# Six edits of a three-block transformer kernel: gain row, mixer order, routing copies, loop rings, stick-breaking order, last norm

## The chip, the cores and the metric

One Trainium2 chip, one core of it. The metric is the device time of one execution in microseconds (us), the median of several runs. The engines are named as in the profile: PE is TensorE, DVE is VectorE, ACT is ScalarE, POOL is GpSimd, SP is SyncE, whose queue carries nearly all transfers.

## What is computed

256 tokens of width 1024, float32 throughout. Two layers, each a mixer and an expert layer with 16384 experts (`peer_ffn`); then one block of two kinds of attention and an MLP.

```python
# layer 0: x += even_mix(norm(x)); x += peer_ffn(norm(x))
# layer 1: x += fox_mix(norm(x));  x += peer_ffn(norm(x))
def rms_norm(x, g):
    return x * lax.rsqrt(jnp.mean(x * x, axis=-1, keepdims=True) + EPS) * g

def even_mix(h, ...):
    p = h @ w_in
    a_val, a_gate, q, k, v, r, glr = jnp.split(p, cuts, axis=-1)
    # gated, a 31-tap causal convolution over the tokens per channel, layer norm, silu
    y_a = conformer_conv(a_val, a_gate, conv_w, conv_b, ln_g, ln_b)
    o = gla_chunked(q, k, v, log_a)              # gated linear attention, 4 heads
    y_b = rms_norm(o, gla_norm_g) * jax.nn.silu(r)
    return jnp.concatenate([y_a, y_b], axis=-1) @ w_out

def peer_ffn(h, wq, keys, u, v):
    q = (h @ wq).reshape(B, S, 8, 2, 128)
    s1, s2 = ...                                 # q against 128 + 128 keys per head
    v1, i1 = lax.top_k(s1, 16); v2, i2 = lax.top_k(s2, 16)
    sc, j = lax.top_k(v1[..., :, None] + v2[..., None, :], 16)
    experts = i1[j // 16] * 128 + i2[j % 16]
    gates = jax.nn.softmax(sc, axis=-1)
    act = jax.nn.gelu(h . u[experts])
    return sum over experts of gates * act * v[experts]

def second_block(x, c, ...):
    mod = jax.nn.silu(c) @ ada_w + ada_b         # shifts, scales and gates
    z = (rms_norm(h) * (1 + scale1) + shift1) @ w_in
    y_a = nsa_attention(...) @ w_up_nsa
    y_b = stick_breaking_attention(q_b, k_b, v_b) @ w_up_sb   # 8 heads
    h = h + gate1 * ((sigmoid(m_a) * y_a + sigmoid(m_b) * y_b) @ w_out)
    u2 = rms_norm(h) * (1 + scale2) + shift2
    return h + gate2 * (square(relu(u2 @ mlp_w1)) @ mlp_w2)
```

## The kernel before

**Products.** Every large product is made of three, of a high and a low part of each operand (`H` and `L`), so that its result is as good as float32. A weight arrives by SP's queue in pieces of 128x1024 (512 KB). `wsplit` (line 110) makes the high part of a piece on ACT (line 90) and the low part on DVE or POOL (line 93). Which of the two is a matter of the ring from which the piece's tiles come: `K.rings` names for each ring, `u`, `v` and at times `w`, the pool and the engine of its low parts. A ring has two tiles of each part (`hu`, `lu`, `hv`, `lv`), so a piece's split waits until PE has finished with the piece two before it in the same ring. By default ring `u` has its low parts on POOL and ring `v` on DVE.

**Expert layer.** All experts are computed, and a matrix `G` (experts by tokens, zero for those not chosen) weighs them. Expert block n is 128 experts; there are 128 blocks in two halves of 64. `first(n)` is 24 matmuls (line 742) and a gelu on ACT (line 745, tile `A`); `gated(n)` multiplies by `G` on DVE (line 750, `AG`) and splits the product (`CH` on ACT, `CL` on DVE); `second(n)` is 12 matmuls per block (lines 764, 765, 768) into four PSUM banks `po`. `RUN` = 40 firsts run ahead of the gated products, and a second follows its gated product by `LAG` = 2 blocks.

**Routing** (line 605) chooses the experts while PE computes queries and, by `ahead`, some of the firsts. `top16` is a chain of DVE operations for each of 8 heads. Behind the last head four ACT copies (line 681, `xe`, 128x2048 each) spread the indices of all eight heads; a softmax and one-hot products on DVE follow (lines 700, 701, 708, 711), and PE transposes their results (lines 705, 713).

**Loop** (line 812). For each half, `spread` builds `G` by one-hot products on DVE (lines 785 to 790: `o1`, `o2`, `og`) and PE; all rings have their low parts on DVE until the loop over n begins, and the rings of before (`u` on POOL) from there on. In some steps of the loop 512 KB of the block's conditioning weights are loaded and multiplied on DVE (line 1035).

**First mixer** (`even`, line 386). The convolution is split: channel group 0 and the first `PART` taps of group 1 run on PE by diagonal matrices, the others on DVE as one operation per tap (line 525). The gated attention's last products (`po`), their norm (`osq`, `oss`) and transposes (line 572) follow the taps. **Norm** (`norm_rows`, line 227): sums of squares (line 207), scaling with the gain row (line 258), transposes on PE (line 261); `leave` and `take` add a mixer's result to `X` (line 318).

**Stick-breaking attention** in `block2`: for each of four pairs of heads `keep_probs` (logits, log-sigmoids `ls`, `lk`), `stick` (sums by a triangular matrix, line 1312, and an exponential) and `sb_values`, with products of the input projection (`wide`) between them; then a sigmoid of the two gates (line 1340, `mg`), two products up and the output product.

The compiler's scheduler orders instructions that aren't pinned, by a priority that follows the order of the code; each engine runs its own list in order.

Of the kernel before, what the change touches and what calls it, by code (L numbers as in the profile page):

```python
# [44 lines left out]
class Kit:  # L45


    def __init__(self, ctx, tc, I):
# [11 lines left out]
        nc.sync.dma_start(self.row, row_bc(I["ev_norm"]))  # L60
# [16 lines left out]
        self.warm(WARM)  # L77
# [149 lines left out]
    def norm_rows(self, g, shift=None, early=(), after=None):  # L227
# [8 lines left out]
        W, outs = [], []  # L236
        first = not self.carry
        rs = [self.rstd(tb, tb > 0) for tb in range(2)] if first else []
        for tb in range(2):
# [7 lines left out]
            if not tb:  # L247
                W = [self.wsplit(*w, (0,), nc.vector) for w in raw]
# [19 lines left out]
            if not tb:  # L268
                for (H, L), w in zip(W, raw):
                    for a, b in zip((H, L), self.wsplit(*w, (1,), nc.vector)):  # L270
                        a.extend(b)
# [110 lines left out]
CONV = (0, 0, 0, 8, 14, 14), (0, 0, 0, 2, 18, 22)  # L382
PART = 12


def even(K, side):
    tc, nc, I = K.tc, K.nc, K.I
    K.table()
    with tc.tile_pool(name="evz", bufs=1) as ez, ExitStack() as stack:
# [159 lines left out]
        K.rings = old  # L549
        last = conv_dve(len(steps))  # L550
# [5 lines left out]
        for tb in range(2):  # L556
            po = pm.tile([128, 4, 128], F, name="pm")
            for h in range(4):
                if tb:
                    nc.tensor.matmul(po[:, h], ATx[:, h], V[0][:, h], start=True, stop=False)  # L560
                nc.tensor.matmul(po[:, h], AT[tb][:, h], V[tb][:, h], start=not tb, stop=True)
            sq = wk.tile([128, 4, 128], F, name="osq")
            ss = wk.tile([128, 4], F, name="oss")
            nc.scalar.activation(sq, po, AF.Square)
            nc.vector.tensor_reduce(ss, sq, axis=AX.X, op=OP.add)
            nc.scalar.activation(ss, ss, AF.Ln, bias=K.eps, scale=1.0 / 128)
            nc.scalar.activation(ss, ss, AF.Exp, scale=-0.5)
            for h in range(4):
                nc.vector.scalar_tensor_tensor(sq[:, h], po[:, h], ss[:, h:h + 1], sr[tb][:, h], op0=OP.mult, op1=OP.mult)
            pt = pm.tile([128, 4, 128], F, name="pm")  # L570
            for h in range(4):
                nc.tensor.transpose(pt[:, h], sq[:, h], K.ident)
# [32 lines left out]
def routing(K, l, grid, rt, new_psum, e1T, e2T, gP, ahead):  # L605
# [31 lines left out]
    q = {}  # L637

    def evac(g, ps):
        q[g] = rt.turn("q", [128, S], bufs=4)  # L640
        nc.scalar.activation(q[g], ps, AF.Copy)
# [23 lines left out]

    qs = K.row[:, 0:512].rearrange("p (a b) -> p a b", b=256)
    nc.scalar.activation(qs, qn, AF.Copy)
    for h in range(1, 8):
        K.gemm_T(I[f"p{l}_wq"], (2 * h - 2, 2 * h), K.hH, K.hL, lambda g, ps: evac(g + 2, ps), psum=pfx)
        ahead(1)  # L670
        if h == 1:
# [5 lines left out]
            best(0)  # L677
        best(h)
    for t in range(2):
        for i in range(2):  # L680
            nc.scalar.activation(xe[:, t, :, i], IX[:, t, i::2, :, None].to_broadcast([128, 8, 16, 16]), AF.Copy)
# [899 lines left out]
```

## Time and profile before

| | |
|---|---|
| median of 3 runs | 2380.89 us (2379.44 to 2382.56) |
| the profiled execution's own time | 2386.93 us |
| its span, first to last instruction | 2385.2 us |
| mean granted TensorE clock | 0.987 |
| busy: PE, DVE, ACT, POOL | 97%, 66%, 53%, 34% of the span |

The device time holds the span and under 2 us around it. The profiled execution is 6 us above the median, so gains read from it are taken off the median, not off its own time. PE is busy nearly throughout; what can be won without taking away matmuls is the time in which it waits, and the time in which its granted clock is half.

### The profile page before, as it was taken

The numbers are of one execution on the slowest core, as the hardware profiler recorded it, in microseconds if no ns is written. First come the engines' busy times: TensorE is split into PE (matmuls) and PEld (weight loads), VectorE is DVE, ScalarE is ACT, GpSimd is POOL, SyncE is SP. The second block draws the span as 40 slices with busy tenths as digits, with TensorE's granted clock in tenths as the row PEclk, the third lists the DMA queues.
The fourth block names the chain that finished last, engine by engine and source line by source line (L and its number), as shares of the span: only waits on it lengthen the run. The fifth ranks groups of instructions, "written<-read, shape, count | busy, mean of one in ns | idle before, by whom it ended". The sixth has DMA issues, their size and how long they took to land.

```text
span 2385.2 us, 43282 instructions
## 1 busy us (share of the span) xinstructions
PE 2310.5 (97%) x16982; PEld 2092.9 (88%) x16982; DVE 1576.8 (66%) x3094; ACT 1260.9 (53%) x2031; POOL 801.7 (34%) x361
## 2 busy tenths in 40 slices
PE   8989899999999999999989999999999999999999
PEld 8879898988998988887989898899899879877997
DVE  5958997556873556644799756688355663657754
ACT  5544555555554555575455455555455554565542
POOL 4228304444003444552840344500244442323000
PEclk9999999999999999999999999999999999999999
DMA  7235446665556665642644576554566565334652
GB/s 248 80 116 182 138 142 218 241 203 188 167 168 206 235 214 194 214 141 70 196 139 147 195 245 206 192 176 154 194 239 225 195 214 177 115 105 152 213 188 94
DMA packets 119529, 425.15 MB, mean 178 GB/s; under 512 B 14170, under 2 KB 17052, under 8 KB 118940
## 3 DMA queue, kind: packets, MB, share of 16 engines
q1 hardware_dynamic: 119324, 422.38, 53.0%
q8 instruction: 133, 2.18, 0.4%
q14 instruction: 72, 0.59, 0.1%
HBM read 421.24 MB, written 2.66 MB: 178 GB/s over the span
## 4 chain that ended last, share of the span: by engine, by line
PE 45%; DVE 5%; issue 1%; ACT 1%; POOL 1%; POOLq 0%; ACTq 0%; DVEq 0%
PE pA L742 13%; PE pA L155 6%; PE po L764 5%; PE po L765 5%; PE po L768 5%; PE pB L155 2%; PE pB L799 1%; PE pA L196 1%; PE pA L197 1%; PE pA L195 1%; PE pB L197 1%; PE pB L195 1%; PE pB L196 1%; POOL lu L93 1%; DVE G L635 1%
## 5 line engine op out<-in xcount | busy, mean ns | idle before, releaser
L93 POOL TENSOR_TENSOR lu<-raw,hu 128x1024 fp32r<-128x1024 f32 x263 | 652.5, 2485 | 1198.0 <-ACT hu L90 1013.2
L90 ACT ACTIVATE hu<-raw 128x1024 fp32r<-128x1024 f32 x352 | 372.1, 1059 | 339.0 <-PE pA L742 251.0
L93 DVE TENSOR_TENSOR lv<-raw,hv 128x1024 fp32r<-128x1024 f32 x306 | 381.7, 1248 | 122.8 <-ACT hv L90 120.2
L90 ACT ACTIVATE hv<-raw 128x1024 fp32r<-128x1024 f32 x336 | 355.6, 1060 | 194.9 <-PE pA L742 81.2
L742 PE MATMUL pA<-hH,hu 128*128 128x256 f32 x1408 | 400.0, 284 | 5.2 <-ACT hu L90 5.2
L93 DVE TENSOR_TENSOR CL<-AG,CH 128x256 fp32r<-128x256 f32 x256 | 213.2, 834 | 288.6 <-PE po L768 167.1
L742 PE MATMUL pA<-hH,lu 128*128 128x256 f32 x1408 | 396.2, 281 | 6.4 <-POOL lu L93 6.1
L742 PE MATMUL pA<-hL,hu 128*128 128x256 f32 x1408 | 395.0, 281 | 0.0
L742 PEld LDWEIGHTS pA<-hH,lu 128*128 128x128 f32 x1408 | 269.6, 191 | 8.0 <-POOL lu L93 7.8
L742 PEld LDWEIGHTS pA<-hH,hu 128*128 128x128 f32 x1408 | 266.4, 189 | 9.2 <-ACT hu L90 6.0
L742 PEld LDWEIGHTS pA<-hL,hu 128*128 128x128 f32 x1408 | 267.4, 190 | 3.5
L90 ACT ACTIVATE CH<-AG 128x256 fp32r<-128x256 f32 x256 | 106.9, 419 | 296.9 <-PE po L765 280.5
L764 PE MATMUL po<-hv,CH 128*128 128x512 f32 x672 | 262.0, 390 | 0.0
L765 PE MATMUL po<-lv,CH 128*128 128x512 f32 x672 | 261.5, 389 | 0.0
L768 PE MATMUL po<-hv,CL 128*128 128x512 f32 x672 | 206.9, 389 | 0.0
L742 PE MATMUL pA<-hH,hv 128*128 128x256 f32 x640 | 184.5, 288 | 14.3 <-ACT A L745 14.3
L742 PE MATMUL pA<-hH,lv 128*128 128x256 f32 x640 | 180.0, 281 | 1.4 <-POOL lv L93 1.4
L742 PE MATMUL pA<-hL,hv 128*128 128x256 f32 x640 | 179.7, 281 | 0.0
L768 PEld LDWEIGHTS po<-hv,CL 128*128 128x128 f32 x672 | 126.2, 188 | 26.3
L764 PEld LDWEIGHTS po<-hv,CH 128*128 128x128 f32 x672 | 126.5, 188 | 22.8
L765 PEld LDWEIGHTS po<-lv,CH 128*128 128x128 f32 x672 | 126.4, 188 | 22.8
L765 PE MATMUL po<-lu,CH 128*128 128x512 f32 x352 | 137.8, 396 | 4.7 <-POOL lu L93 4.7
(637 smaller groups left out, 5241.6 us busy)
## 6 DMA issues: line engine op xcount, KB each, us to landing
raw<-in_p_u_dram SPq DMA_DIRECT2D x256, 512.0 KB, 3.6
raw<-in_p_v_dram SPq DMA_DIRECT2D x256, 512.0 KB, 4.2
raw<-in_b_m_dram SPq DMA_DIRECT2D x64, 512.0 KB, 3.4
raw<-in_b_ada_dram SPq DMA_DIRECT2D x48, 512.0 KB, 3.3
raw<-in_b_wT_dram SPq DMA_DIRECT2D x33, 512.0 KB, 3.4
raw<-in_p_wq_dram SPq DMA_DIRECT2D x32, 512.0 KB, 3.8
raw<-in_od_wT_dram SPq DMA_DIRECT2D x17, 512.0 KB, 3.4
raw<-in_ev_wT_dram SPq DMA_DIRECT2D x13, 512.0 KB, 6.8
```

The lines of the kernel that those rows point to most:

```text
L90: i = nc.scalar.activation(H, src, AF.Copy)
L93: return (eng or nc.vector).tensor_sub(L, src, H.bitcast(F))
L155: nc.tensor.matmul(out, a, b[:, k], start=c == 0, stop=c == 3 * kd - 1)
L195: nc.tensor.matmul(po[tb][c], x, h, start=i == 0 and k == 0, stop=False)
L196: nc.tensor.matmul(po[tb][c], x, l, start=False, stop=False)
L197: nc.tensor.matmul(po[tb][c], y, h, start=False, stop=last and k == 3)
L635: nc.vector.max_index(io[:, 8:16], vo[:, 8:16], w)
L742: nc.tensor.matmul(ps, a[:, ks], b[:, k], start=c == 0, stop=c == 23)
L764: nc.tensor.matmul(po[tb][dh], CH[:, ts], H[:, ds], start=n == 0, stop=False)
L765: nc.tensor.matmul(po[tb][dh], CH[:, ts], L[:, ds], start=False, stop=False)
L768: nc.tensor.matmul(po[tb][dh], CL[:, ts], H[:, ds], start=False, stop=n == 127)
L799: nc.tensor.matmul(pg[:, t], o2[:, t // 2, :, t % 2], og[:, t // 2, c, :, t % 2], start=c == 0, stop=c == 1)
```

## The change

Six edits. They take away no product of the computation.

1. **Start.** The first norm's gain row is read once (4 KB, ACT's queue) and spread over 128 partitions by two matmuls with a row of ones and two DVE copies, where a 512 KB transfer on SP's queue did it. The 50 small matmuls that fill the start are split 36 and 14.
2. **First mixer.** PE takes 19 taps of channel group 1, where it took 12, so DVE has 7 fewer. The attention's products, squares, sums and scaling stand before the last taps; its transposes and splits stay behind them.
3. **Routing.** The copies of six heads (`wider(0, 6)`) are issued behind the last query's evacuation, and those of the last two at the end.
4. **Loop.** The rings keep their low parts on DVE for the first four steps of each half; the second weights of blocks 62 and 63 come from ring `v`, where they came from `u`.
5. **Stick-breaking.** `stick` and `sb_values` stand a step later, and all rings have their low parts on DVE from there to the output product.
6. **Last norm** (`sooner`). The early weights are split whole ahead of the sums of squares.

```diff
-        nc.sync.dma_start(self.row, row_bc(I["ev_norm"]))
+        ones = self.scr[1][0:1, 0:128]
+        nc.vector.memset(ones, 1.0)
+        nc.scalar.dma_start(self.row[0:1], I["ev_norm"])
...
-        self.warm(WARM)
+        self.warm(WARM - 14)
+        for d in range(0, D, 512):
+            p = self.ps.tile([128, 512], F, name="pA")
+            nc.tensor.matmul(p, ones, self.row[0:1, d:d + 512], start=True, stop=True)
+            nc.vector.tensor_copy(self.row[:, d:d + 512], p)
+        self.warm(14)
...
-    def norm_rows(self, g, shift=None, early=(), after=None):
+    def norm_rows(self, g, shift=None, early=(), after=None, sooner=False):
...
+        if sooner:
+            self.pinning = True
+            W = [self.wsplit(*w, eng=nc.vector) for w in raw]
+            self.pinning = False
...
-CONV = (0, 0, 0, 8, 14, 14), (0, 0, 0, 2, 18, 22)
-PART = 12
+CONV = (0, 0, 0, 8, 14, 0), (0, 0, 0, 2, 18, 22)
+PART = 19
...
         K.rings = old
+        po = [pm.tile([128, 4, 128], F, name="pm") for _ in range(2)]
+        for tb in range(2):
+            for h in range(4):
+                if tb:
+                    nc.tensor.matmul(po[tb][:, h], ATx[:, h], V[0][:, h], start=True, stop=False)
+                nc.tensor.matmul(po[tb][:, h], AT[tb][:, h], V[tb][:, h], start=not tb, stop=True)
+        sq = [wk.tile([128, 4, 128], F, name="osq") for _ in range(2)]
+        for tb in range(2):
+            ss = wk.tile([128, 4], F, name="oss")
+            nc.scalar.activation(sq[tb], po[tb], AF.Square)
+            conv_dve(4)
+            pin(nc.vector.tensor_reduce(ss, sq[tb], axis=AX.X, op=OP.add))
+            nc.scalar.activation(ss, ss, AF.Ln, bias=K.eps, scale=1.0 / 128)
+            nc.scalar.activation(ss, ss, AF.Exp, scale=-0.5)
+            conv_dve(4)
+            for h in range(4):
+                pin(nc.vector.scalar_tensor_tensor(sq[tb][:, h], po[tb][:, h], ss[:, h:h + 1], sr[tb][:, h],
+                                                   op0=OP.mult, op1=OP.mult))
         last = conv_dve(len(steps))
         conv_pe(len(taps))
...
+    def wider(a, b):
+        for t in range(2):
+            for i in range(2):
+                nc.scalar.activation(xe[:, t, a:b, i], IX[:, t, 2 * a + i:2 * b:2, :, None]
+                                     .to_broadcast([128, b - a, 16, 16]), AF.Copy)
...
+        if h == 7:
+            with K.tc.issue_after(last[0].ins):
+                wider(0, 6)
         best(h)
-    for t in range(2):
-        for i in range(2):
-            nc.scalar.activation(xe[:, t, :, i], IX[:, t, i::2, :, None].to_broadcast([128, 8, 16, 16]), AF.Copy)
+    wider(6, 8)
...
-                late = n % HALF >= HALF - RUN - LAG and n // 2 % 2
+                late = n % HALF >= HALF - RUN - LAG and n // 2 % 2 and n != HALF - 2
...
             ahead(RUN)
-            K.rings = old
             if ada:
                 ada.open()
             for n in range(h0, h0 + HALF):
+                if n == h0 + 4:
+                    K.rings = old
                 gated(n)
...
+            K.rings = {r: (p, nc.vector) for r, (p, e) in K.rings.items()}
             for i in range(7):
                 if i < 4:
                     wide(9 + 2 * i, 2)
+                elif i < 6:
+                    wide(21 + 2 * i, 2)
+                if 2 <= i:
+                    stick(i - 2) if i < 6 else None
+                if i < 4:
                     keep_probs(i)
-                if 0 < i < 5:
-                    stick(i - 1)
-                if 4 <= i < 6:
-                    wide(21 + 2 * i, 2)
-                if 1 < i < 6:
-                    sb_values(i - 2)
+                if 3 <= i:
+                    sb_values(i - 3)
...
-    early, = K.norm_rows(g2, mod[:, 24:32], [(I["b2_m10"][:, 0], "u")], flat(I["b2_m1"][:, 0:2]))
+    early, = K.norm_rows(g2, mod[:, 24:32], [(I["b2_m10"][:, 0], "u")], flat(I["b2_m1"][:, 0:2]), True)
```

The change moves line numbers: line 90 becomes 98, 93 becomes 101, 681 becomes 688, 697 becomes 723, 745 becomes 771, 750 becomes 776, 785 to 790 become 811 to 816, 1035 becomes 1062.

**ACT at the end of the first routing.** Before, from the last query's neighbours on (`G<-pA` are query evacuations, `G<-G` the spread copies, `A<-pA` gelus):

```order
L90 ACTIVATE hu<-raw 128x1024
L745 ACTIVATE A<-pA 128x256
L681 ACTIVATE G<-G 128x8x256 x4
L697 ACT_TABLE_LOAD
L697 ACTIVATE G<-G 128x256
L745 ACT_TABLE_LOAD
L745 ACTIVATE A<-pA 128x256 x2
L90 ACTIVATE hu<-raw 128x1024
L90 ACTIVATE hv<-raw 128x1024 x2
```

Now:

```order
L688 ACTIVATE G<-G 128x6x256 x2
L771 ACTIVATE A<-pA 128x256
L688 ACTIVATE G<-G 128x6x256 x2
L688 ACTIVATE G<-G 128x2x256 x2
L771 ACTIVATE A<-pA 128x256
L688 ACTIVATE G<-G 128x2x256
L98 ACTIVATE hu<-raw 128x1024
L688 ACTIVATE G<-G 128x2x256
L771 ACTIVATE A<-pA 128x256
L98 ACTIVATE hu<-raw 128x1024
L98 ACTIVATE hv<-raw 128x1024
L723 ACT_TABLE_LOAD
```

The four whole copies stood in one block ahead of two table loads; six heads' copies now stand in pieces between gelus, and the last two heads' smaller ones between splits.

**DVE at the first loop's start.** Before, from the last one-hot product of the first half's `spread` on (the numbers tell tiles apart; `og_7009` and `og_7055` belong to the second half's `spread`):

```order
L790 TENSOR_TENSOR og_4593<-o1_4591,gP_1516 128x4x128 x2
L787 TENSOR_TENSOR o2_7008<-grid_1517,e2T_1515 128x1024
L785 TENSOR_TENSOR o1_7007<-grid_1517,e1T_1514 128x512
L790 TENSOR_TENSOR og_7009<-o1_7007,gP_1516 128x4x128 x2
L785 TENSOR_TENSOR o1_7053<-grid_1517,e1T_1514 128x512
L787 TENSOR_TENSOR o2_7054<-grid_1517,e2T_1515 128x1024
L790 TENSOR_TENSOR og_7055<-o1_7053,gP_1516 128x4x128 x2
L750 TENSOR_TENSOR AG_4669<-A_1766,G_1513 128x256
L750 TENSOR_TENSOR AG_4714<-A_1942,G_1513 128x256
L1035 SCALAR_TENSOR_TENSOR raw_4745,modp_1506<-raw_4745,pB_4663 128x512
L93 TENSOR_TENSOR CL_4668<-AG_4669,CH_4667 128x256
L93 TENSOR_TENSOR CL_4713<-AG_4714,CH_4712 128x256
```

Now:

```order
L816 TENSOR_TENSOR og_4619<-o1_4617,gP_1538 128x4x128 x2
L101 TENSOR_TENSOR lu_4704<-raw_4699,hu_4703 128x1024
L811 TENSOR_TENSOR o1_7033<-grid_1539,e1T_1536 128x512
L813 TENSOR_TENSOR o2_7034<-grid_1539,e2T_1537 128x1024
L816 TENSOR_TENSOR og_7035<-o1_7033,gP_1538 128x4x128 x2
L811 TENSOR_TENSOR o1_7079<-grid_1539,e1T_1536 128x512
L813 TENSOR_TENSOR o2_7080<-grid_1539,e2T_1537 128x1024
L101 TENSOR_TENSOR lu_4708<-raw_4701,hu_4707 128x1024
L776 TENSOR_TENSOR AG_4695<-A_1788,G_1535 128x256
L776 TENSOR_TENSOR AG_4740<-A_1964,G_1535 128x256
L1062 SCALAR_TENSOR_TENSOR raw_4771,modp_1528<-raw_4771,pB_4689 128x512
L1062 SCALAR_TENSOR_TENSOR raw_4771,modp_1528<-raw_4771,pB_4690 128x512
```

Two low parts of ring `u` stand among the one-hot products, where POOL made them, and one product of the second half (`og` of `o1_7079`) stands later.

**ACT at the second half's start of the first layer.** Before, between the last firsts of the run ahead and the first gated product (`CH`):

```order
L745 ACTIVATE A<-pA 128x256 x3
L90 ACTIVATE hu<-raw 128x1024
L745 ACTIVATE A<-pA 128x256
L90 ACTIVATE hu<-raw 128x1024
L745 ACTIVATE A<-pA 128x256
L90 ACTIVATE hv<-raw 128x1024
L745 ACTIVATE A<-pA 128x256
L90 ACTIVATE hu<-raw 128x1024
L90 ACTIVATE hv<-raw 128x1024
L90 ACTIVATE CH<-AG 128x256
```

Now:

```order
L771 ACTIVATE A<-pA 128x256
L98 ACTIVATE hv<-raw 128x1024
L771 ACTIVATE A<-pA 128x256
L98 ACTIVATE hv<-raw 128x1024
L771 ACTIVATE A<-pA 128x256
L98 ACTIVATE hu<-raw 128x1024
L771 ACTIVATE A<-pA 128x256
L98 ACTIVATE hu<-raw 128x1024
L771 ACTIVATE A<-pA 128x256
L98 ACTIVATE hu<-raw 128x1024
L771 ACTIVATE A<-pA 128x256
L98 ACTIVATE CH<-AG 128x256
```

The two splits of ring `v` come first now, and the three of ring `u` stand behind them, the last of them next to `CH`.

## Rows read from the trace of the kernel before

**Rows 1.** Page, part 1: busy time, share of the span and instructions.

```profile
PE 2310.5 (97%) x16982; PEld 2092.9 (88%) x16982; DVE 1576.8 (66%) x3094; ACT 1260.9 (53%) x2031; POOL 801.7 (34%) x361
```

**Rows 2.** TensorE's waits, whole span: total us, times, longest us.

```profile
PE pA L742 <- ACT A L745: 14.3, 2, 7.2
PE pA L742 <- POOL lu L93: 6.1, 4, 2.5
PE pA L742 <- ACT hu L90: 5.2, 2, 2.7
PE po L765 <- POOL lu L93: 4.7, 4, 1.3
PE pB L1312 <- DVE lk L1305: 4.3, 2, 2.2
PE pA L261 <- DVE raw L258: 4.0, 1, 4.0
PE pm L572 <- DVE osq L569: 3.7, 4, 3.1
PE pA L196 <- POOL lu L93: 2.2, 2, 1.5
PE pA L742 <- POOL lv L93: 1.4, 1, 1.4
PE pA L155 <- POOL lu L93: 1.4, 1, 1.4
```

**Rows 3.** Windows, TensorE: length, busy (matmuls), granted clock, DMA share, GB/s.

```profile
249.50:256.30 6.80, 4.25 (x20) 0.50 0.00 0
362.75:368.16 5.41, 5.41 (x47) 1.00 0.58 193
368.45:381.70 13.25, 8.32 (x36) 0.74 0.63 210
540.00:600.00 60.00, 60.00 (x267) 1.00 0.58 193
729.60:756.50 26.90, 22.41 (x146) 0.94 0.51 174
2123.20:2127.00 3.80, 3.80 (x9) 0.55 0.64 224
```

**Rows 4.** Timeline of VectorE at the start: start us, length us, instruction.

```profile
8.25 0.69 DVE L207 SCALAR_TENSOR_TENSOR hH<-X 128x512 fp32r<-128x512 f32 x1 [1.19 <-DMA X<-in_x_dram]
10.25 0.75 DVE L258 SCALAR_TENSOR_TENSOR raw<-X,ss,raw 128x512 f32<-128x512 f32 x1 [1.30 <-DMA raw<-in_ev_norm_dram]
```

**Rows 5.** Timeline of VectorE in the first mixer and behind it.

```profile
110.30 8.68 DVE L525 SCALAR_TENSOR_TENSOR acc<-u,cp,acc 128x256 f32<-128x256 f32 x20
158.41 0.68 DVE L318 TENSOR_TENSOR X<-X,pB 128x512 f32<-128x512 f32 x1
```

**Rows 6.** Timeline at the end of the first routing, four engines.

```profile
241.26 7.31 ACT L681 ACTIVATE G<-G 128x2048 bf16<-128x2048 uint32 x4 [1.60 <-DVE G L635]
255.88 6.80 POOL L93 TENSOR_TENSOR lv<-raw,hv 128x1024 fp32r<-128x1024 f32 x2
260.34 2.61 DVE L701 TENSOR_TENSOR G<-G 128x256 f32<-128x256 f32 x1
263.01 0.33 PE L705 MATMUL pB<-cid,G 128*128 128x128 f32 x1 [0.53 <-DVE G L701]
```

**Rows 7.** Timeline of VectorE at both loop starts of the first layer.

```profile
363.02 2.84 DVE L790 TENSOR_TENSOR og<-o,gP 128x512 f16<-128x512 f16 x2
366.84 0.75 DVE L790 TENSOR_TENSOR og<-o,gP 128x512 f16<-128x512 f16 x2
367.51 0.75 DVE L750 TENSOR_TENSOR AG<-A,G 128x256 f32<-128x256 f32 x2
725.36 1.23 DVE L93 TENSOR_TENSOR lu<-raw,hu 128x1024 fp32r<-128x1024 f32 x1 [1.50 <-ACT hu L90]
```

**Rows 8.** Timeline of ScalarE behind stick-breaking.

```profile
2144.64 3.62 ACT L1340 ACTIVATE mg<-mg 128x4096 f32<-128x4096 f32 x1
```

More of the change, by code (lines that the diff above doesn't have):

```diff
@@ L247, in norm_rows @@
             if not tb:
-                W = [self.wsplit(*w, (0,), nc.vector) for w in raw]
+                W = W or [self.wsplit(*w, (0,), nc.vector) for w in raw]
             elif after is not None:
@@ L267, in norm_rows @@
                 self.chain = self.split(self.hH[:, k:k + 4, ts], self.hL[:, k:k + 4, ts], p)
-            if not tb:
+            if not tb and not sooner:
                 for (H, L), w in zip(W, raw):
@@ L556, in even @@
         for tb in range(2):
[L557 to L569, printed above, removed]
             pt = pm.tile([128, 4, 128], F, name="pm")
             for h in range(4):
-                nc.tensor.transpose(pt[:, h], sq[:, h], K.ident)
+                nc.tensor.transpose(pt[:, h], sq[tb][:, h], K.ident)
             ts = slice(tb * 128, tb * 128 + 128)
@@ L635, in top16 @@
         nc.vector.max_index(io[:, 8:16], vo[:, 8:16], w)
-    q = {}
+    q, last = {}, [None]
     def evac(g, ps):
         q[g] = rt.turn("q", [128, S], bufs=4)
-        nc.scalar.activation(q[g], ps, AF.Copy)
+        last[0] = nc.scalar.activation(q[g], ps, AF.Copy)
     def best(h):
```

## The prediction

> **What bounds the kernel now.** I read the page's busy shares first: PE is busy for 2310.5 us, 97% of the span [rows 1]. No engine beside it comes near, so the kernel ends when PE's list ends, and an edit is worth what it takes from PE's waits or from the time at half clock. So the list of PE's waits came next [rows 2]: the reader is to see that one wait is met twice at 7.2 us, once per layer (14.3 in all, behind ACT's `A`), that the loop starts give four kinds (L742 behind `hu` 5.2, behind `lu` 6.1, L765 behind `lu` 4.7), and that the rest are single waits of 1 to 4 us. Then the windows around them, for the granted clock [rows 3]: it is 1.00 in long stretches and 0.50 right behind a long wait (249.50 to 256.30), which is the lower of its two levels. A wait so costs twice, once itself and once in matmuls that then run at half speed. Last came the timelines of the other engines in these places [rows 4 to 8], since they say what is late next.
>
> The unit prices of PE at full clock: 47 firsts' matmuls in 5.41 us, 0.115 each, and 267 of the second kind in 60.00 us, 0.225 each [rows 3].
>
> **Start.** DVE's first scaling (L258) waited 1.30 us for the gain row at 10.25; the last sum of squares before it began at 8.25 and took 0.69 [rows 4]. With a 4 KB row it can begin right there, 1.3 earlier. The two spreading matmuls and copies lie under the wait for X. PE waited 4.0 us here [rows 2], filler matmuls aside, so the gain is between 0 and 4.0; I take 1.5, near the one wait that is named. **−1.5.**
>
> **First mixer.** DVE's taps cost 8.68/20 = 0.434 us each [rows 5]; seven fewer are 3.0. PE's wait for L569's scaling, 3.7 in four pieces [rows 2], goes, since the scaling now stands before the last taps. PE gets seven taps more, each a 128x256 product in plain float32, for which I show no row: not under 7 x 0.115 = 0.8 by the firsts' price, and I leave the 3.7 us as the room that they fill. Against it: the order of the next norm changes, all four additions to X now stand ahead of its scaling, two of them being those that stood at 158.41 (0.68 each, 1.4) behind it [rows 5]. DVE sets this end, so 3.0 − 1.4 = 1.6 is the low estimate, 3.0 + 3.7 − 1.4 = 5.3 the high one, and nothing is the bound if PE's extra taps turn out to be in its way. **−3.**
>
> **Start of the routing.** The first layer's waits of 1.4 behind `lv` and 1.4 behind `lu` [rows 2] go if the early splits come sooner, as the earlier end of the norm and ACT's order suggest; bounds 0 to 2.8, I take **−2**.
>
> **End of the routing.** Before, ACT's copies hold it for 7.31 us from 241.26, and PE's firsts can't go on, since their gelus and splits stand behind: the wait of 7.2 [rows 2, 6]. Then the clock falls to 0.50 until 256.30, with 4.25 us of busy time in that window, half of which, 2.1, would not be there [rows 3]. So up to 7.1 + 2.1 = 9.2 us per layer could come back. I don't believe that it does: what PE needs after these firsts are the transposes behind DVE's chain. That chain was not waiting for ACT's block alone. Its gate product L701 began at 260.34 and took 2.61, while POOL made low parts for 6.80 us from 255.88 [rows 6]; PE reached its transposes just then, with a last wait of 0.53 at 263.01 [rows 6]. If PE runs its firsts early, it stands before the transposes early, and waits there for a DVE chain of the same length with the same number of POOL operations beside it. The wait moves, with its clock. The worth is between −9.2 and +2 (one more DVE operation held up by one POOL operation, below); I take **0** for both layers, nearest to the row at 260.34.
>
> What POOL costs DVE here can be read from another place: two `og` products took 2.84 us at 363.02 beside a POOL low part, and 0.75 at 366.84 alone [rows 7]: 2.1 for one blocked operation. The Trainium skill, page "SBUF — State Buffer", section "Who interferes with whom", says that the port pair which DVE and GpSimd share is an exclusive lock, and that a DVE instruction with two inputs in SBUF contends with a GpSimd instruction that reads SBUF. The trace agrees, with these 2.1 us. By that rule each low part of POOL that falls into the chain of one-hot products lengthens it; by my sum the count of them stays the same; one more in each layer would make the sum 4.2 us worse.
>
> **First loop start, both layers.** The window from 368.45 to 381.70 holds 24 firsts' and 12 seconds' matmuls: 24 x 0.115 + 12 x 0.225 = 5.5 us of work in 13.25. So 7.8 us are lost, at a clock of 0.74 [rows 3]: the waits behind `hu` (2.7) and `lu` (2.5) [rows 2], and the half clock behind them. The cause is in DVE's row: the first `AG` came only at 367.51, behind one-hot products of the second half and POOL's hold at 363.02 [rows 7]; `CH` behind it on ACT, then `hu`, then `lu` on POOL. Now the low parts are made by DVE, 1.23 us alone [rows 7] against 6.80/2 = 3.4 on a POOL beside a busy DVE [rows 6], and no POOL operation holds the one-hot products (2.1 saved per occasion). But they stand in DVE's own list: by the order shown, two `lu` come ahead of `AG`, and the next one, `lu` of the following piece, behind two conditioning products of 0.68 each and two `CL`. ACT's `CH` and `hu` come behind `AG` as before. I count: the wait behind `lu` goes, half of that behind `hu` stays, and of the 2.6 at half clock half stays: 5 of 7.8. The bounds are 2 (one POOL hold saved, no more) and 7.8. **−5 per layer, −10.**
>
> **Second loop start, both layers.** The window from 729.60 to 756.50 holds 120 whole firsts' matmuls and 24 seconds': 120 x 0.115 + 24 x 0.225 = 19.2 us in 26.90, so 7.7 are lost [rows 3], in waits (L765 behind `lu`, 4.7 in both layers [rows 2], and others) and at clock 0.94. The weights of blocks 62 and 63 came from ring `u`, whose two tiles the firsts still held, with low parts on POOL; now they come from ring `v`, free by then, with low parts on DVE at 1.23, and DVE has little to do here: the product at 725.36 began when its high part was there [rows 7]. So nearly all comes back; the firsts' own wait there, about 0.6 (L742 behind `lu`, 6.1 less two of 2.5, for two layers [rows 2]), may stay. Bounds 2.4 (the seconds' waits behind `lu` alone) and 7.7; I take 6.5. **−13.**
>
> **Stick-breaking.** PE waited twice for `lk`, 4.3 us [rows 2], and ran at 0.55 from 2123.20 for 3.80 us, which is 1.7 us lost [rows 3]: 6.0. With `stick` a step later a whole `wide` product lies between. Against it: the gates' sigmoid, 3.62 us on ACT at 2144.64 [rows 8], stands behind the last `sb_values`, which is now a step later, inside the next product; PE has a few PSUM banks to fill meanwhile, and then waits, 1 to 3.6 us. I take 2.5. **−3.5**; bounds 0 and −6.
>
> **Output product.** The waits of L196 behind POOL's `lu`, 2.2 in two [rows 2], go with low parts on DVE, with some of a wait for `hu` before it. **−2.5**; bounds −1 and −3.5.
>
> **Last norm.** The early splits now precede the sums of squares, but their tiles come free only when the output product has read them, so they hold the squares as much as they help later; the wait for the scaling there is 1.5 [rows 2], which bounds it either way. **0.**
>
> **Sum.** 1.5 + 3 + 2 + 0 + 10 + 13 + 3.5 + 2.5 + 0 = 35.5 us. The profiled execution took 2386.9, so it would take 2351.4; the median is 6.0 lower, 2380.9, and so the forecast is 2345.4.
>
> **Rivals.**
>
> *The routing's wait goes for good.* If DVE's chain gets ahead too, because the copies of six heads are no longer in its way, 9.2 per layer come back: 18.4 more, 2327. For it speaks the size of the wait; against it that PE arrived at the transposes with almost no time to spare.
>
> *The loop starts are mostly given back.* DVE runs its list in order, and has the one-hot products, `AG`, `CL`, conditioning products and now low parts in one list. If the low bounds hold, 2 and 2.4 per layer, the loops give 9 and not 23: 2360.
>
> *The chain at the routing's end grows until the change is slower.* PE's earlier firsts free tiles earlier, and POOL's low parts for them fall among more of DVE's one-hot products, each held up by 2.1. It decides from 35.5/2.1 = 17 blocked operations more, eight or nine per layer, on top of those there now; with 20 such, 2387. Against it: only eight firsts are issued at this point, so few low parts are left to fall there.
>
> *Little happens.* Each wait is replaced by the next engine's, as at the routing's end: within 0.2% of 2380.9.
>
> **Chances.** Forecast 0.55; the routing's gain 0.14; the loops given back 0.24; little happens 0.04; slower 0.03. Differences under 0.2%, 4.8 us, can't be told from none here. So faster 0.93, same 0.04, slower 0.03. The range 2325 to 2366 takes in the first two rivals with a little beside them (the loops given back and stick-breaking and start at nothing: 2365; the last two cases and the ends of the first two lie outside).
>
> **What would show it.** PE's list of waits: L742 behind `A` no longer 7 us, but PE waiting at the transposes (L731, the former L705) behind DVE for as long: right on the routing. The loop windows: from `spread`'s end the first 36 matmuls in 8 us and not 13; the second start without waits behind `lu` on L791. Waits behind `lk` gone and one behind the gates' sigmoid in the product up. I am wrong if POOL's low parts still stand ahead of PE at the loops, if the granted clock stays low there though the waits are gone, or if the routing's stall disappears altogether.

## The result and the profile after

The changed kernel's median is 2349.71 us, against 2381.72 us before: 32.0 us less, a ratio of 0.9862 with an interval of 0.9843 to 0.9881. The forecast was 2345.4 in a range of 2325 to 2366. One run of the changed kernel, at a mean clock of 0.746 throughout, is left out of the ratio but counts in its median, which is 2348.28 over the three others. A second set of runs of the same kernel on another chip (e5 below) gave 0.9851, 0.9836 to 0.9866.

The profiled execution's span is 2344.8 us, 40.4 less than the one shown of before. That is more than the medians differ by: the profiled execution of before was 5 us above its median, that of after 3 below its own.

First the page's part 1 of the changed kernel, in the columns of [rows 1]:

```profile
PE 2293.3 (98%) x17000; PEld 2080.4 (89%) x17000; DVE 1595.6 (68%) x3124; ACT 1262.6 (54%) x2046; POOL 714.3 (30%) x327
```

Then TensorE's waits after, the view of [rows 2]:

```profile
PE pB L731 <- DVE G L727: 21.2, 2, 10.6
...
PE pA L163 <- DVE mg L1375: 2.5, 1, 2.5
...
PE pA L768 <- ACT A L771: 1.7, 2, 0.8
...
PE pA L768 <- DVE lu L101: 0.6, 2, 0.3
```

The loop starts are clean: of the firsts' waits behind low parts, 6.1 us in [rows 2], 0.6 are left behind VectorE's and 0.2 behind GpSimd's, and the waits of L765 behind GpSimd (4.7) and those behind `lk` (4.3) are no longer in the list. The routing's wait of 14.3 behind ACT is 1.7. In its place stand 21.2 us at the transposes, 10.6 in each layer, and this is the largest wait that is left.

Windows of the changed kernel, columns as in [rows 3]:

```profile
242.00:257.00 15.00, 3.57 (x28) 0.79 0.53 178
359.93:367.55 7.62, 7.11 (x59) 1.00 0.76 263
```

The first is the wait at the transposes; the clock falls in it, and how long it stays down is read under e1. The second is the first loop start: its 59 matmuls, up to one of the first seconds, take 7.62 us and hold no half clock, where the 36 of [rows 3] took 13.25 at 0.74.

To divide the difference, here is the same matmul in both traces at eleven places (us from each span's start):

| place | before | after | lead of after |
|---|---|---|---|
| routing's queries, layer 0 | 186.16 | 177.48 | 8.7 |
| first matmul after its transposes, `spread` begun | 277.22 | 272.87 | 4.3 |
| a matmul of the first seconds, first loop start | 379.43 | 367.55 | 11.9 |
| firsts after blocks 62 and 63, second loop start | 753.47 | 734.30 | 19.2 |
| first matmul after the transposes, layer 1 | 1231.07 | 1215.94 | 15.1 |
| first loop start, layer 1 | 1345.41 | 1322.88 | 22.5 |
| second loop start, layer 1 | 1719.61 | 1689.62 | 30.0 |
| product up, behind the gates’ sigmoid | 2148.76 | 2116.14 | 32.6 |
| output product, last rows | 2176.81 | 2140.57 | 36.2 |
| MLP | 2227.73 | 2189.89 | 37.8 |
| MLP, 55 us on | 2283.55 | 2243.61 | 40.0 |

So the routing's end costs: 4.4 us in layer 0 and, from 19.2 to 15.1, 4.1 in layer 1. Each loop start gives between 7.3 and 7.6. Half of the lead in the first row, 4.4 us, is there at 60 us from the start. The profiled execution of e1, whose start is the changed kernel's, is 4.0 behind there too, and that of e11, which takes the start back, only 1.0: most of the 4.4 is a difference of executions and not of the change.

### The profile page after: what moved, and what is told of

Its sections match the earlier page's. It is cut to its first block, busy times and chain, and to the rows that moved or that the text cites. A ratio compares the mean times of both kernels' runs of the same rounds, so it can differ in the third digit from the quotient of the medians.

```text
span 2344.8 us, 43309 instructions
## 1 busy us (share of the span) xinstructions
PE 2293.3 (98%) x17000; PEld 2080.4 (89%) x17000; DVE 1595.6 (68%) x3124; ACT 1262.6 (54%) x2046; POOL 714.3 (30%) x327
## 4 chain that ended last, share of the span: by engine, by line
PE 45%; DVE 5%; ACT 1%; issue 0%; DMA 0%; POOL 0%; SPq 0%; ACTq 0%; POOLq 0%; DVEq 0%
PE pA L768 14%; PE pA L163 5%; PE po L791 5%; PE po L794 5%; PE po L790 5%; PE pB L163 2%; PE pB L825 1%; PE pA L204 1%; PE pA L205 1%; PE pA L203 1%; PE pB L205 1%; PE pB L204 1%; PE pB L203 1%; DVE G L653 1%; DVE G L650 1%; DVE G L651 1%
## 5 line engine op out<-in xcount | busy, mean ns | idle before, releaser
L101 POOL TENSOR_TENSOR lu<-raw,hu 128x1024 fp32r<-128x1024 f32 x229 | 569.0, 2488 | 1164.9 <-ACT hu L98 1046.3
L101 DVE TENSOR_TENSOR CL<-AG,CH 128x256 fp32r<-128x256 f32 x256 | 205.9, 805 | 258.0 <-PE po L794 132.0
L790 PE MATMUL po<-hv,CH 128*128 128x512 f32 x688 | 267.7, 390 | 0.0
L791 PE MATMUL po<-lv,CH 128*128 128x512 f32 x688 | 267.5, 389 | 0.0
L794 PE MATMUL po<-hv,CL 128*128 128x512 f32 x688 | 211.9, 389 | 0.0
L101 DVE TENSOR_TENSOR lu<-raw,hu 128x1024 fp32r<-128x1024 f32 x119 | 145.5, 1223 | 62.5 <-ACT hu L98 61.6
L790 PEld LDWEIGHTS po<-hv,CH 128*128 128x128 f32 x688 | 129.0, 188 | 23.1
```

The lines of the kernel that those rows point to most:

```text
L101: return (eng or nc.vector).tensor_sub(L, src, H.bitcast(F))
L790: nc.tensor.matmul(po[tb][dh], CH[:, ts], H[:, ds], start=n == 0, stop=False)
L791: nc.tensor.matmul(po[tb][dh], CH[:, ts], L[:, ds], start=False, stop=False)
L794: nc.tensor.matmul(po[tb][dh], CL[:, ts], H[:, ds], start=False, stop=n == 127)
```

## The experiments

Each is an edit of the changed kernel. Ratios are to the kernel before, run beside it on the same chip; the changed kernel's own are 0.9862 and, in e5, 0.9851.

**e5, the changed kernel again.** No edit.

> The changed kernel once more, unaltered, on the same chip as the three beside it, as the mark that they are compared with. All theories: 2346 to 2352, a ratio of 0.985 to 0.988 to the kernel before.

Measured: 2348.57, ratio 0.9851 (0.9836 to 0.9866). This is the mark below.

**e1, the routing's copies as before.**

```diff
-        if h == 7:
-            with K.tc.issue_after(last[0].ins):
-                wider(0, 6)
         best(h)
-    wider(6, 8)
+    wider(0, 8)
```

> The changed kernel with the index copies of all eight heads back behind the last head, as before; everything else as changed. Theory A (held-up operations): the early copies let GpSimd's low parts start beside VectorE's small operations, five of which then took 2.3 to 2.5 us each, and the routing's end became 4.2 to 4.4 us longer per layer than before: about 8.5 us faster than the changed kernel, near 2341, with a wait of 7.1 us for ACT's gelu in each layer back and the wait at the transposes down from 10.6 to under 1. Theory B (the stall only moved, as the prediction had it): within 2 us of the changed kernel.

Measured: 2335.80, ratio 0.9798 (0.9785 to 0.9812), 0.5% below the changed kernel: some 13 us by the ratios, with some 3 us of width on either side of each, and 4.0 and 4.6 us in the two layers in the trace. The edit of the routing is a loss, so theory B falls. VectorE in the changed kernel, between its last sorting operations and the transposes:

```profile
239.48 2.48 DVE L712 TENSOR_SCALAR G<-G 128x256 uint32<-128x256 uint32 x1
241.88 2.47 DVE L713 TENSOR_SCALAR G<-G 128x256 uint32<-128x256 uint32 x1
244.39 2.50 DVE L714 SCALAR_TENSOR_TENSOR G<-G 128x256 bf16<-128x256 uint32 x1
246.92 2.32 DVE L715 TENSOR_SCALAR G<-G 128x256 uint32<-128x256 uint32 x1
249.16 2.42 DVE L716 TENSOR_SCALAR G<-G 128x256 uint32<-128x256 uint32 x1
251.50 1.21 DVE L734 TENSOR_TENSOR G<-G 128x2048 bf16<-128x2048 bf16 x1
```

and GpSimd there:

```profile
236.87 4.94 POOL L101 TENSOR_TENSOR lu<-raw,hu 128x1024 fp32r<-128x1024 f32 x2 [6.42 <-ACT hu L98]
241.77 4.83 POOL L101 TENSOR_TENSOR lv<-raw,hv 128x1024 fp32r<-128x1024 f32 x2
246.57 4.86 POOL L101 TENSOR_TENSOR lu<-raw,hu 128x1024 fp32r<-128x1024 f32 x2
```

The reader is to see that five operations in a row take as long as a GpSimd operation each, 2.3 to 2.5 us, and that the first one after GpSimd's end at 251.43 takes 1.21, as a large product does alone. In e1, the same two engines (its lines are three lower):

```profile
242.41 0.29 DVE L709 TENSOR_SCALAR G<-G 128x256 uint32<-128x256 uint32 x1
242.61 0.29 DVE L710 TENSOR_SCALAR G<-G 128x256 uint32<-128x256 uint32 x1
...
248.37 3.24 DVE L734 TENSOR_TENSOR G<-G 128x2048 bf16<-128x2048 bf16 x1
251.54 2.36 DVE L723 TENSOR_SCALAR G<-G 128x16 f32<-128x16 f32 x1
...
254.95 2.62 DVE L724 TENSOR_TENSOR G<-G 128x256 f32<-128x256 f32 x1
```

```profile
247.89 2.64 POOL L101 TENSOR_TENSOR lu<-raw,hu 128x1024 fp32r<-128x1024 f32 x1 [11.46 <-ACT hu L98]
250.49 6.80 POOL L101 TENSOR_TENSOR lv<-raw,hv 128x1024 fp32r<-128x1024 f32 x2
```

Here ACT's block of copies keeps the high parts back, GpSimd starts 5.5 us after the first of these operations, where it was 2.6 us ahead of it, and three operations are held up ahead of the transposes, not five. The changed kernel has two holds more, 4.3 us, but two of the large one-hot products (L734 and L737 in its numbering) fewer ahead of the gate product, 2.3: its chain, from the operation at 238.88 to the gate product's end at 256.49, takes 17.6 us, and that of e1 15.5. So 2.1 of the loss are VectorE's. The other half is TensorE's clock. Its rows at the transposes, first in the changed kernel, then in e1:

```profile
256.55 0.48 PE L731 MATMUL pB<-cid,G 128*128 128x128 f32 x1 [10.58 <-DVE G L727]
256.81 3.62 PE L739 MATMUL pB<-G 128*128 128x128 bf16 x32
```

```profile
257.83 0.27 PE L728 MATMUL pB<-cid,G 128*128 128x128 f32 x1
257.94 1.95 PE L736 MATMUL pB<-G 128*128 128x128 bf16 x32
```

and the stretch at half clock in each (windows, columns as in [rows 3]):

```profile
250.66:260.90 10.24, 4.35 (x36) 0.50 0.25 90
```

```profile
246.64:252.85 6.21, 6.21 (x29) 0.50 0.21 71
```

In e1, as in the kernel before, TensorE stops ahead of its last firsts, runs most of them at half clock while VectorE's chain goes on, and reaches the transposes with 0.5 us or less to wait: the half clock there costs nothing. In the changed kernel TensorE stops right at the transposes, and the first 4.35 us of work behind the wait run at 0.50, some 2.1 us that nothing covers. By the same matmuls in both traces the loss is 1.9 us up to the transposes and 2.1 behind them; in layer 1 it is 2.1 and 2.5.

The rule that I had weighed (the Trainium skill, page "SBUF — State Buffer", section "Who interferes with whom") is that of an exclusive lock on the shared port pair. The trace agrees in that each operation held up ends 0.2 to 0.3 us after a GpSimd operation does. But I had weighed it for instructions with two SBUF inputs, and four of these five are `TENSOR_SCALAR` with one; the same section says that `tensor_scalar` can enter the modes that use both ports, and so contend.

**e2, the low parts at the routing's end on VectorE.** The early copies stay.

```diff
         K.gemm_T(I[f"p{l}_wq"], (2 * h - 2, 2 * h), ...)
+        if h == 7:
+            K.rings = {r: (K.ring, nc.vector) for r in "uv"}
         ahead(1)
```

> The changed kernel, with the low parts of the firsts issued from the last head of the routing on made by VectorE and not by GpSimd. Theory A: no GpSimd operation is beside VectorE's chain, so its small operations take 0.3 us again and the transposes begin some 5 to 6 us earlier, after three or four low parts of 1.22 us: the wait at the transposes falls from 10.6 to about 5 us per layer, 8 to 11 us faster than the changed kernel. Theory B (VectorE is simply full here, whoever makes the low parts): the low parts take on VectorE what they cost on GpSimd, and the wait stays within 2 us of 10.6.

Measured: 2329.99, ratio 0.9777 (0.9764 to 0.9791), 0.74% below the changed kernel, or 17 us; the transposes come 7.2 us earlier in layer 0 than in the changed kernel and 6.9 in layer 1 on top of that (the lead grows from 7.2 to 14.1 there). That is more than the 8 to 11 us I had expected; the clock (below) is part of why. VectorE in e2:

```profile
241.29 1.21 DVE L101 TENSOR_TENSOR lu<-raw,hu 128x1024 fp32r<-128x1024 f32 x1
...
242.98 0.28 DVE L714 TENSOR_SCALAR G<-G 128x256 uint32<-128x256 uint32 x1
243.18 0.28 DVE L715 TENSOR_SCALAR G<-G 128x256 uint32<-128x256 uint32 x1
243.38 1.22 DVE L101 TENSOR_TENSOR lu<-raw,hu 128x1024 fp32r<-128x1024 f32 x1
244.52 0.42 DVE L716 SCALAR_TENSOR_TENSOR G<-G 128x256 bf16<-128x256 uint32 x1
```

The small operations are at 0.28 again. VectorE makes the low parts itself in 1.2 us, and loses 2.1 us when GpSimd makes them. Theory B (VectorE is full anyway) falls. The wait is now three pieces of 1.2 to 1.8 us per layer behind gelus and low parts, with 0.4 at the transposes, and the granted clock stays at 1.00 until the last 1.5 us of the span, so the 2.1 us per layer at half clock go too. So the early copies were a good idea with the wrong engine beside them.

**e8, e2 with seven firsts and one between the transposes.**

```diff
-        ahead(5 - 2 * t)
+        ahead(7 - 6 * t)
```

> As e2 (low parts of the firsts at the routing's end on VectorE), and with seven firsts ahead of the first block's transposes and one ahead of the second's, where it is five and three. If TensorE still runs out of firsts while VectorE's chain ends, two more cover it, and it is 2 to 5 us faster than e2, near 2326. Rival: in e2 TensorE waited for the low parts and gelus themselves, not for want of firsts; then two low parts more stand in VectorE's list ahead of the one-hot products, and it is the same as e2 or 2 to 5 us slower.

Measured: 2329.50, ratio 0.9775 (0.9762 to 0.9788): the same as e2, as the rival said. TensorE did not want for firsts.

**e3, the rings of before from the loop's start.**

```diff
             ahead(RUN)
+            K.rings = old
...
-                if n == h0 + 4:
-                    K.rings = old
```

> The changed kernel with the rings of before from the loop's start on, that is without the four steps with low parts on VectorE; block 62 still in ring v. My account puts nearly the whole gain at the first loop starts (7.5 us per layer) on this edit: 13 to 15 us slower than the changed kernel, with waits behind the low parts at the first starts back. Rival: the gain at the first loop start comes with the moved order of the list, not with the engine of the low parts: under 5 us slower.

Measured: 2359.96, ratio 0.9901 (0.9886 to 0.9916), 0.5% or 12 us slower than the mark, a little under the range that I had given. In the trace it is 14.4 us behind by the second start of layer 1; the two first starts hold some 12 of that, and each second start 0.9. Its waits:

```profile
PE pA L768 <- POOL lu L101: 6.1, 6, 2.2
PE pA L768 <- ACT hu L98: 5.2, 2, 2.7
```

These are the figures of [rows 2] again. So the engine of the low parts is most of the first starts' gain, some 12 of 15 us; the rest is not shown.

**e4, blocks 62 and 63 in ring u.**

```diff
-                late = ... and n // 2 % 2 and n != HALF - 2
+                late = ... and n // 2 % 2
```

> The changed kernel with the second weights of blocks 62 and 63 back in ring u; low parts on VectorE for the first four steps as changed. If the ring is what counts at the second starts, the waits for hu and lu at those two blocks return in part, and it is 6 to 14 us slower. If the engine of the low parts is what counts, it is within 3 us of the changed kernel.

Measured: 2352.02, ratio 0.9861 (0.9845 to 0.9876); the interval is too wide to tell it from the mark. The trace tells more: `PE po L790 <- ACT hu` waits 3.6 us in four pieces that the changed kernel does not have, the longest 1.6, and e4 falls 3.6 us behind at the second start of layer 0 and 2.5 in layer 1. Ring and engine both count at the second starts, but what e3 and e4 lose there, 4.5 and 3.4 us per layer, is about half of the 7.4 that both together gave. The wait of the seconds behind GpSimd's low parts (4.7 in [rows 2]) is in neither list, so either edit alone removes it; that the rest of the gain is this wait and the clock behind it is argued, since no run takes both edits back.

**e6, the first mixer as before** (12 taps, attention's products behind the taps).

```diff
-CONV = (0, 0, 0, 8, 14, 0), (0, 0, 0, 2, 18, 22)
-PART = 19
+CONV = (0, 0, 0, 8, 14, 14), (0, 0, 0, 2, 18, 22)
+PART = 12
...
-        po = [pm.tile([128, 4, 128], F, name="pm") for _ in range(2)]
...
         for tb in range(2):
+            po = pm.tile([128, 4, 128], F, name="pm")
...
```

> The changed kernel with the first mixer of before (12 taps of group 1 on TensorE, attention's products behind the taps). My sum gave the mixer 3 us and the start of the routing 2 us, together 5: then it is 4 to 6 us slower than the changed kernel, with the wait of 3.1 us for the scaled squares back and the mixer's output product some 5 us later, of which the added order of the next norm gave back 2 to 3. Rival: the two traces' lead at that place (9 us) belongs to the first mixer in full: 8 to 9 us slower.

Measured: 2354.66, ratio 0.9880 (0.9865 to 0.9895), 0.3% or 7 us slower, with 4.0 us in the trace at the routing's queries. Three waits are back:

```profile
PE pm L584 <- DVE osq L581: 4.1, 4, 3.1
...
PE pA L762 <- POOL lv L101: 1.4, 1, 1.4
PE pA L163 <- POOL lu L101: 1.3, 1, 1.3
```

The output product comes 4.2 us later, the first products of the next norm's two halves only 1.7 and 0.6: the added order (all additions to X first) gives back what I had taken for it, and the two waits at the routing's start return the rest. The sum of 5 stands.

**e7, the order of stick-breaking as before**, low parts still on VectorE.

```diff
                 if i < 4:
                     wide(9 + 2 * i, 2)
-                elif i < 6:
+                    keep_probs(i)
+                if 0 < i < 5:
+                    stick(i - 1)
+                if 4 <= i < 6:
                     wide(21 + 2 * i, 2)
-                if 2 <= i:
-                    stick(i - 2) if i < 6 else None
-                if i < 4:
-                    keep_probs(i)
-                if 3 <= i:
-                    sb_values(i - 3)
+                if 1 < i < 6:
+                    sb_values(i - 2)
```

> The changed kernel with the order of stick-breaking of before; low parts stay on VectorE there. By my sum the order was worth 6.0 less a new wait of 2.5 for the gates' sigmoid: 3 to 4 us slower than the changed kernel, both waits of about 2.1 behind lk back, and the wait of 2.5 behind mg gone. Rival: with low parts on VectorE and not on GpSimd the waits behind lk are gone anyway (lk was late because VectorE was held up): then it is 1 to 3 us faster than the changed kernel, since only the wait behind mg goes.

Measured: 2346.29, ratio 0.9844 (0.9829 to 0.9859): the same as the mark or a little faster, and no wait behind `lk` at all. The rival is right. VectorE in e7 where before the two `lk` were late:

```profile
2071.15 0.96 DVE L1329 TENSOR_TENSOR lk<-lsm,z 128x768 f32<-128x768 f32 x1
2072.02 1.22 DVE L101 TENSOR_TENSOR lu<-raw,hu 128x1024 fp32r<-128x1024 f32 x1
2073.16 0.68 DVE L1332 TENSOR_TENSOR lk<-lk,cc 128x512 f32<-128x512 f32 x1
```

In the kernel before, the first of these and, elsewhere, the other were long, each beside a low part on GpSimd:

```profile
2100.11 2.98 DVE L1302 TENSOR_TENSOR lk<-lsm,z 128x768 f32<-128x768 f32 x1
2119.54 2.72 DVE L1305 TENSOR_TENSOR lk<-lk,cc 128x512 f32<-128x512 f32 x1
```

It was VectorE that was held up, and a step more of distance was not needed. In the trace the old order loses 0.8 us within stick-breaking and gains 2.5 at the gates' sigmoid.

**e9, the new order with ring u's low parts on GpSimd.**

```diff
-            K.rings = {r: (p, nc.vector) for r, (p, e) in K.rings.items()}
             for i in range(7):
```

> The changed kernel with the default rings (ring u's low parts on GpSimd) from stick-breaking to the output product; the order of stick-breaking stays as changed. If the engine of the low parts is what freed TensorE there (e7), the output product's waits behind GpSimd's low parts return, about 2.7 with their clock, and stick-breaking, whose order is a step longer, is hurt less than before the change: 3 to 7 us slower than the changed kernel. Rival: the longer step covers VectorE's holds by itself, and only the output product's waits return: 2 to 3 us slower.

Measured: 2356.06, ratio 0.9898 (0.9876 to 0.9920), 0.5% or 11 us slower, 8.4 us in the trace, over the upper end that I had given. From its list of waits:

```profile
PE pA L204 <- POOL lu L101: 2.2, 2, 1.5
...
PE pB L1339 <- DVE lk L1332: 1.4, 1, 1.4
```

A wait behind `lk` is there even with the longer step, though less than the 4.3 of [rows 2] in the old order, and the output product loses 5.1 us (from 2.3 behind at the product up to 7.4, matmul for matmul), its waits and a stretch at 0.50 behind them.

**e11, the gain row by 512 KB on SP's queue.**

```diff
-        nc.scalar.dma_start(self.row[0:1], I["ev_norm"])
+        nc.sync.dma_start(self.row, row_bc(I["ev_norm"]))
...
-        self.warm(WARM - 14)
-        ...                      # matmuls with ones, copies, warm(14)
+        self.warm(WARM)
```

> The changed kernel with the gain row of the first norm as 512 KB on SP's queue again. My sum gave the start 1.5 us; the traces showed the first scaled rows 1.2 to 3.4 us earlier. Then it is 1 to 4 us slower, with the wait of about 4 us for the first scaling back and the clock at half behind it. Rival: the input's arrival sets the start and varies by as much: no difference that lasts beyond the first 60 us.

Measured: 2348.36, ratio 0.9857 (0.9836 to 0.9878): nothing, as the rival said. VectorE at the start, the changed kernel first, then e11:

```profile
6.19 0.69 DVE L84 COPY raw<-pA 128x512 f32<-128x512 f32 x1 [5.10 <-PE pA L83]
7.05 0.69 DVE L84 COPY raw<-pA 128x512 f32<-128x512 f32 x1 [0.17 <-PE pA L83]
...
7.88 0.69 DVE L215 SCALAR_TENSOR_TENSOR hH<-X 128x512 fp32r<-128x512 f32 x1
...
9.10 0.75 DVE L270 SCALAR_TENSOR_TENSOR raw<-X,ss,raw 128x512 f32<-128x512 f32 x1
```

```profile
6.22 0.69 DVE L207 SCALAR_TENSOR_TENSOR hH<-X 128x512 fp32r<-128x512 f32 x1
...
8.97 0.75 DVE L262 SCALAR_TENSOR_TENSOR raw<-X,ss,raw 128x512 f32<-128x512 f32 x1 [1.37 <-DMA raw<-in_ev_norm_dram]
```

In e11 the input had come by 6.2, and the sums of squares began; the wait for the gain row is there with 1.37, but the scaling starts at 8.97, earlier than the changed kernel's 9.10. There the two copies of the row stand ahead of the sums in VectorE's list and hold them until 7.88. The one wait is exchanged for the other.

**e12, the last norm's splits as before.**

```diff
-    ..., flat(I["b2_m1"][:, 0:2]), True)
+    ..., flat(I["b2_m1"][:, 0:2]))
```

> The changed kernel without the early splits ahead of the last norm's sums. My sum gave this 0: within 1.5 us of the changed kernel. Rival: the splits' place is what removed the half clock at this norm (6.8 us of it before, none after), and 2 to 4 us are lost without it.

Measured: 2347.85, ratio 0.9855 (0.9836 to 0.9874): the same, as the sum had it. The rival was right that a stretch at half clock comes back at this norm (3.4 us at 0.50 from 2165.10, behind a wait of 1.5 for the scaling), but it costs nothing in the end: without the early splits the norm's first products come 1.6 us sooner, and the wait and the clock take back just that.

**e10, e2 and e7 together.** The edits are theirs.

> The changed kernel with low parts on VectorE at the routing's end (e2) and the order of stick-breaking of before (e7). If the two are apart, as their places in the trace say, the gains add: e2's 0.7 to 0.8% and e7's 0 to 0.1%, 2326 to 2330, and the traces show neither the wait at the transposes nor that behind mg. Rival: e7's gain is noise, and it equals e2 within 1 us.

Measured: 2333.04, ratio 0.9783 (0.9764 to 0.9802), no different from e2 and over the 2326 to 2330 expected. The wait behind `mg` is gone from its list, and the timed runs do not show it. In the trace e10 is 1.5 us ahead of e2 at the product up and loses more than that at the last norm, where 10 us run at 0.50 (two stretches from 2141.90 to 2155.50) and e2 has none; why the clock falls there in one and not in the other is open. The best kernels here are e2 and e8, at a ratio of 0.978 to the kernel before, 0.7 to 0.8% below the changed one.

## Why the prediction was right, and where it was not

The time lay in the range, 4.3 us above the forecast. The sum was near partly by luck: the loop starts gave more than I had put down, and the routing took most of that back.

- **Start, 1.5.** Wrong: nothing. The step that failed is "it can begin right there, 1.3 earlier": I had looked at what the scaling waits for and not at what the change puts ahead of the sums, though I wrote that the copies "lie under the wait for X". They did in the trace of before, where X was late, and do not when it is early (e11).
- **First mixer and start of the routing, 3 + 2.** Right, by e6, for the two together: 4.0 in the trace, 7 by the ratios with their width, and each of the three named waits. No run takes the taps and the order of the products back one by one.
- **End of the routing, 0.** The stall moved to the transposes, as I said, but it did not keep its length: −4.4 and −4.1 in the two layers, beyond my bound of 2. Two steps failed. One is "for a DVE chain of the same length with the same number of POOL operations beside it": what counts is how many VectorE operations are held up ahead of the transposes, three before (e1 shows the same) and five after, and the chain is 2.1 longer. The other is "The wait moves, with its clock", put at nothing: before, the half clock (249.50 to 256.30) lay under VectorE's chain, since TensorE still had 0.53 to wait at the transposes, so with that chain as it was neither the 7.1 nor the 2.1 that I counted was there to be won; moved behind the transposes, the half clock costs 2.1 to 2.5 that nothing covers (e1). My slower rival named the first of these and its price of 2.1; I gave it the size that would turn the whole result, and not one that it could have.
- **First loop starts, 10.** Mis-sized: 7.6 + 7.4 = 15.0, the high end of my bounds. The half of the wait that I thought would stay behind `AG` did not: with no GpSimd operation beside it, VectorE reached the first `AG` early enough, and e3 takes some 12 of the 15 back. Its row after, 7.1 us earlier than that of [rows 7], where all else had a lead of 4.3:

```profile
360.37 0.76 DVE L776 TENSOR_TENSOR AG<-A,G 128x256 f32<-128x256 f32 x2
```

- **Second loop starts, 13.** Measured 7.3 + 7.5 = 14.8, a little more. In mechanism it is shown in part: the waits behind `lu` are gone, e4 (ring) and e3 (engine) together undo about half of the gain, and for the other half there is no run.
- **Stick-breaking, 3.5.** The lead grows from 30.0 to 32.6, so 2.6 since the loop. In between 1.6 us are lost at a stretch at 0.50 from 1974.40, in products of `block2` that the change does not touch; the place itself gave 4.3, from 28.3 to 32.6. The new wait behind the gates' sigmoid came as said, 2.5 us. But the step "with `stick` a step later a whole `wide` product lies between" is not what removed the waits behind `lk`: e7 has the old order and no such wait, e9 the new order and one of 1.4. The engine of the low parts did it; with that engine the order added 0.8 and cost 2.5 (e7).
- **Output product, 2.5.** 3.6 in the leads, 5.1 in e9, with its clock: somewhat too small.
- **Last norm, 0.** Right by e12. The wait of 1.5 for which the sum names [rows 2] is this row of the same view, further down:

```profile
PE pB L261 <- DVE raw L258: 1.5, 1, 1.5
```

- The last 2.1 us of the profiles' difference lie in the MLP, which the change does not touch (below). They are no gain: the profiled execution of e5, the same kernel, loses 2.8 us against the changed kernel's from the last norm on.

Without the routing's loss of 8.5 us the measured gain of 32.0 would have been 40.5, and the sum of 35.5 some 5 too small; the errors cancelled in part. The rival of the loops given back had the wrong sign of my doubt: I feared VectorE's list, and at the loop starts it ran ahead of that of before, since a low part costs it 1.2 us and being held up by one 2.1.

## What to carry to other kernels

Before a step is called free because another engine does it, look for the operations of the first engine beside it that took a multiple of their usual time: in this kernel a GpSimd product of two SBUF operands cost VectorE 2.1 us of waiting, and VectorE made the same product in 1.2. When a change lets one engine start earlier, count what its operations now fall beside, ahead of the next point where the bounding engine waits; their total number doesn't tell. Ask too where a stretch at half clock lies: here it cost nothing while VectorE's chain was still running, and some 2 us per layer behind the wait for that chain's end. Of a bundle of edits in one place, take each back by itself: here the order of stick-breaking and the gain row did nothing, and the routing's copies cost more than a loop start gave, 8.5 us against 7.5, while the sum looked right.

## What the runs showed that I had not expected

- Small operations suffer as large ones do: five of 0.29 to 0.43 us (in e1 the first two took 0.29) took 12.0 us, from 239.48 to 251.5: VectorE and GpSimd took turns there, one operation each. VectorE's sorting operations beside the same GpSimd operation were not held: this one, in the changed kernel, lies inside GpSimd's stretch from 236.87 and took 0.24:

```profile
238.35 0.24 DVE L652 MAX8 G<-G 128x8 f32<-128x100 f32 x1
```

- TensorE's pace differed between executions at the same granted clock. The same 515 matmuls of the MLP's first product, in the changed kernel and then in e10 (windows, columns as in [rows 3]):

```profile
2179.90:2238.05 58.15, 58.15 (x515) 1.00 0.61 195
```

```profile
2163.58:2224.00 60.42, 60.42 (x515) 1.00 0.63 185
```

TensorE waits in neither, and the code is the same there. What sets this 4% is open. It is a reason to compare places in a trace by their leads at the nearest matmuls and not from the far end of the span.
